# Delta keys without TensorE: their sums of squares and their turned block by VectorE and DRAM

## The chip, the cores and the metric

The kernel runs on one core of a Trainium2 chip. The metric is the device time of one execution in microseconds (us). An execution computes the whole two-layer trunk for one sequence of 256 positions. Besides timed executions there is one that was profiled; its trace gives the start and the length of every instruction on the engines TensorE (PE, with its weight loads as PEld), VectorE (DVE), ScalarE (ACT), GpSimd (POOL) and SyncE (SP).

## What is computed

The reference is a decoder trunk of two layers. Each layer is a half-step SwiGLU, a layer norm, three mixers side by side (a gated delta rule, sliding-window attention, attention to a memory), a merge, a layer norm, another half-step SwiGLU and a layer norm. The change lies in the delta rule, whose queries, keys and values come out of a short causal convolution and a SiLU; queries and keys are then scaled to unit length per position and head:

```python
def deltanet_branch(q, k, v, b, a, z, conv_w, a_log, dt_bias, norm_w):
    qkv = jax.nn.silu(causal_depthwise_conv(jnp.concatenate([q, k, v], axis=-1), conv_w))
    q, k, v = jnp.split(qkv, 3, axis=-1)          # each then (B, 256, 4 heads, 128)
    q = q * lax.rsqrt(jnp.sum(q * q, -1, keepdims=True) + RMS_EPS)
    k = k * lax.rsqrt(jnp.sum(k * k, -1, keepdims=True) + RMS_EPS)
    beta = jax.nn.sigmoid(b)
    g = -jnp.exp(a_log) * jax.nn.softplus(a + dt_bias)
    o = gated_delta_rule(q, k, v, g, beta)
    ...
```

The delta rule works on chunks. Its decays come from cumulative sums of `g` along the sequence, and the state that passes from the first block of 128 positions to the second is a product of the first block's keys, with positions as rows, and its values.

## The kernel before

All activations stand with channels on the 128 partitions and positions along the free axis, so the keys are `kT`, a tile of 128 channels x 4 heads x 256 positions. Where the kernel needs positions on the partitions, it turns 128x128 blocks.

**Weights.** All weights come as one stream of units of 128x1024 float32. For each unit SP starts a load into `raw` (four buffers, line 115). `split` (line 124) then makes two rounded parts of it: ScalarE casts it to `whi`, and VectorE subtracts, giving `wlo`, each in a ring of five buffers. Every product of a float32 pair is made of three TensorE matmuls of such parts (`mm3`). So each unit costs ScalarE one cast and VectorE one subtraction, and a buffer of the ring comes free when TensorE has used its unit. In the stage of this change a unit is 24 matmuls.

**Order.** From `mixers` on, TensorE's instructions are pinned to the order of the program's text (`pinned`, line 131). The other engines' orders are made by a scheduler when the program is built, from dependencies and priorities; each engine then takes its instructions strictly in that order. `weave(work, steps)` (line 145) lets the matmuls of `work` run unit by unit and calls the functions of `steps[n]` after the n-th unit; this places their TensorE instructions between those units. `tc.issue_after(x)` asks the scheduler for a place behind `x`.

**The stage of the change.** `conv(seg, dst)` (line 545) projects one segment in two halves of two units each. For each half, ScalarE scales and VectorE adds three shifted products (line 553) for each of two channel blocks, and ScalarE applies SiLU (line 554), whose last instruction is kept in `silu[0]`. The segments are run in the order keys, queries, values. After the third unit of the queries `tok_k` (line 577) is called:

- `tok` (line 566) turns all four heads of one 128-position block of the keys on TensorE into a PSUM tile `sm`, four transposes (line 137) for each of two blocks;
- `sumsq` (line 572) squares that on ScalarE and sums over channels on VectorE, into `ssq[:, 0]`, one number per position and head;
- the first block's turned keys are also copied by ScalarE into `ktok`;
- then `rk2` (the reciprocal of the sums) and `kn` (their square root's inverse, by small VectorE steps, lines 261 to 266) follow.

After the convolutions come the small operations of the gates: `be` (sigmoid; ScalarE's exponential at line 651 is asked to stand behind `silu[0]`, the last SiLU), `cS` (`be` times `rk2`), and a series for the softplus in `spz` and `spp` (lines 657 to 674), which ends in `g` (line 676). TensorE goes on with the projection of the cross-attention's queries and of the sliding window's keys (split into `swk`, line 866) and queries. In the latter, after its first unit, stands `decay` (line 680): its two small matmuls read `g`, and VectorE then scales `ktok` (line 689). `spread`, `products` and the recurrence follow; `rec_s1` reads `ktok`.

**What exists already for queries and values.** The queries' sums of squares are made without TensorE: `leave_q` (line 618) squares with ScalarE, turns 32x32 squares with VectorE, sums, and sends the partial sums (16 KB) to DRAM and back in four slices, whose total `land_q` takes. The values are turned by `leave_v` and `back_v`: VectorE turns 32x32 squares, four transfers put the squares in place in DRAM, and one brings the block back, with the channels in the order of squares (a, head, i) in place of (head, a, i). These transfers are started by POOL.

Of the kernel before, what the change touches and what calls it, by code (L numbers as in the profile page):

```python
# [13 lines left out]
AF = mybir.ActivationFunctionType  # L14
# [3 lines left out]
P = 128  # L18
# [20 lines left out]
def tile_trunk(ctx, tc, x, xT, mem, memT_, wst, lnp, memln, cvw, rows, cst, out):  # L39
# [33 lines left out]
    def sm():  # L73
        return T(psS, [P, 512], "sm")
# [61 lines left out]
    def transpose(*a):  # L136
        return pe(nc.tensor.transpose(*a))  # L137
# [386 lines left out]
    def mixers(l, hT, mkT, mv_, post):  # L524
# [91 lines left out]
        turned_v, sums_q = [], []  # L616

        def leave_q():
            part = T(p2, [P, 4, 8], "oqs")
            for tb in range(2):  # L620
                sq = T(p2, [P, 512], "t2", bufs=4)
                nc.scalar.activation(sq.rearrange("p (q h j) -> p q h j", q=4, h=4), squares(qT, tb), AF.Square)
                z = T(p2, [P, 512], "t2", bufs=4)
                nc.vector.transpose(z, sq)
                nc.vector.tensor_reduce(part[:, :, tb * 4:tb * 4 + 4], z.rearrange("p (q h i) -> p q h i", q=4, h=4), axis=AX.X, op=ALU.add)
            d = T(pd, [4, 32, 4, 8], "tq")
            nc.gpsimd.dma_start(d.rearrange("a j t x -> (a j) t x"), part)
            sums_q.append(T(p2, [P, 4, 8], "oqr"))
            for t in range(4):
                nc.gpsimd.dma_start(sums_q[0][32 * t:32 * t + 32], d[:, :, t].rearrange("a j x -> j a x"))  # L630

        def land_q():
            nc.vector.tensor_reduce(ssq[:, 1].rearrange("p t h -> p (t h)"), sums_q[0].rearrange("p a x -> p x a"), axis=AX.X, op=ALU.add)
# [46 lines left out]
        def decay():  # L680
# [342 lines left out]
        def branch(n, o):  # L1023
# [36 lines left out]
            8: [double, lambda: held(leave_q)]})  # L1060
        weave(branch(1, oS), {
            1: [double],
            2: [rec_v0],
# [178 lines left out]
```

## Time and profile before

| | us |
|---|---|
| median of 3 runs | 1273.09 (1271.39 to 1273.2) |
| the profiled execution | 1271.84 |
| its span, first to last instruction | 1270.1 |
| the 16 transposes of the keys, mean of one | 0.27 |
| reduction of one block's squares (line 575), x4 | 0.67 |
| copy of the turned block (line 582), x2 | 0.59 |

The page of a profile gives first the busy time of each engine, then slices of the span, the DMA queues, the chain of work that ended last, and the costliest groups. A row of the timeline gives the start and the length in us, the engine, the line, the operation, the tiles (written <- read), shapes, the count of merged instructions and, in brackets, how long the engine stood idle before it and what ended that. Neighbouring instructions of an engine overlap a little, so distances from start to start say more than lengths. A row of windows gives a stretch, its length, and for each engine the busy time in it with the count of instructions, then the granted TensorE clock, the DMA engines' busy share and GB/s.

### The profile page before, as it was taken

The page shows a single profiled execution, that of the slowest core. Times are in us where ns is not written, and L with a number is a line of the kernel's source. Part 1 is how long each engine was busy: PE and PEld are TensorE (multiplying, and loading weights), DVE is VectorE, ACT ScalarE, POOL GpSimd, SP SyncE. Part 2 cuts the span into 40 slices and gives each one's busy share as a digit, 9 for nine tenths or more (in the row PEclk, how much of TensorE's full clock was granted, in tenths as well). Part 3 has the DMA queues.
Part 4 walks back from the last instruction along what each step waited for, and adds up shares of the span by engine and source line. Part 5 has one row for each costly group of instructions (what it writes and reads, how often), then busy time and mean ns, then how long its engine had stood idle before and what let it go on. Part 6 is the DMA issues. An engine that isn't in the chain of part 4 may idle for free.

```text
span 1270.1 us, 18774 instructions
## 1 busy us (share of the span) xinstructions
PE 1258.1 (99%) x6916; PEld 1070.9 (84%) x6916; DVE 871.3 (69%) x1284; ACT 661.5 (52%) x982; POOL 221.0 (17%) x395
## 2 busy tenths in 40 slices
PE   9999999999999999999999999999999999999997
PEld 7888889999878888888888888899987788888886
DVE  6678576886667776665666665759776588766565
ACT  6456444655664544454454554455646654454441
POOL 1233000002331102221012220000023401122100
PEclk9999999999999999999999999999999999999999
DMA  8988765655554648787668887566554456578771
GB/s 293 322 265 286 249 210 160 205 179 137 164 151 150 240 139 258 243 242 220 215 208 246 256 255 216 178 185 212 162 158 133 134 189 226 174 248 243 240 231 74
DMA packets 78795, 263.56 MB, mean 208 GB/s; under 512 B 12528, under 2 KB 13968, under 8 KB 78704
## 3 DMA queue, kind: packets, MB, share of 16 engines
q1 hardware_dynamic: 66320, 232.40, 56.5%
q0 software_dynamic: 12240, 29.84, 8.7%
q8 instruction: 54, 0.88, 0.3%
q14 instruction: 37, 0.30, 0.1%
q10 hardware_dynamic: 144, 0.13, 0.0%
HBM read 247.48 MB, written 14.85 MB: 207 GB/s over the span
## 4 chain that ended last, share of the span: by engine, by line
PE 94%; DVE 3%; DMA 2%; ACT 1%; issue 1%; SPq 0%; DVEq 0%; ACTq 0%
PE acc L134 83%; PE at L134 3%; PE sm L134 3%; DMA raw<-in_wst_dram 2%; PE sm L137 1%; DVE wlo L125 1%; PE acc L335 1%; PE acc L332 1%; PE at L137 1%; PE acc L333 1%; ACT whi L125 1%; DVE h L291 0%; DVE h L296 0%; DVE h L418 0%; DVE bnst L277 0%
## 5 line engine op out<-in xcount | busy, mean ns | idle before, releaser
L125 DVE TENSOR_TENSOR wlo<-raw,whi 128x1024 fp32r<-128x1024 f32 (+2 forms) x405 | 487.1, 1210 | 277.0 <-ACT whi L125 275.0
L125 ACT CAST whi<-raw 128x1024 fp32r<-128x1024 f32 (+2 forms) x405 | 413.7, 1029 | 403.5 <-PE acc L134 314.8
L134 PE MATMUL acc<-whi,hT 128*128 128x512 f32 (+1 forms) x1824 | 563.1, 386 | 0.0
L134 PEld LDWEIGHTS acc<-whi,hT 128*128 128x128 f32 x1824 | 340.5, 188 | 68.9 <-issue 1.6
L134 PE MATMUL acc<-wlo,hT 128*128 128x512 f32 (+1 forms) x912 | 350.5, 384 | 0.1
L134 PE MATMUL acc<-whi,u 128*128 128x512 f32 x812 | 259.6, 392 | 0.0
L134 PEld LDWEIGHTS acc<-wlo,hT 128*128 128x128 f32 x912 | 171.6, 188 | 33.4 <-DVE wlo L125 0.9
L134 PEld LDWEIGHTS acc<-whi,u 128*128 128x128 f32 x812 | 152.3, 188 | 32.0 <-DVE u L125 0.5
L134 PE MATMUL acc<-wlo,u 128*128 128x512 f32 x406 | 158.2, 390 | 0.0
L362 POOL DMA_DIRECT2D tr<-t x176 | 96.0, 552 | 306.4 <-DVE t L356 299.4
L134 PE MATMUL acc<-hT,whi 128*128 128x256 f32 x672 | 121.8, 284 | 0.0
L134 PEld LDWEIGHTS acc<-hT,whi 128*128 128x128 f32 x672 | 104.7, 192 | 0.0
L134 PE MATMUL acc<-hT,wlo 128*128 128x256 f32 x336 | 95.1, 283 | 0.0
L134 PEld LDWEIGHTS acc<-wlo,u 128*128 128x128 f32 x406 | 76.3, 188 | 15.5
L134 PEld LDWEIGHTS acc<-hT,wlo 128*128 128x128 f32 x336 | 64.4, 192 | 0.0
L363 POOL DMA_DIRECT2D pt<-tr x44 | 25.0, 568 | 197.3 <-DMA tr<-t 151.6
L353 ACT ACTIVATE t<-acc 128x256 f32<-128x256 f32 x88 | 33.3, 379 | 37.1 <-PE acc L134 36.9
L134 PE MATMUL acc<-u,u 128*128 128x512 f32 x186 | 46.4, 394 | 0.0
L354 DVE TENSOR_TENSOR t<-t,acc 128x256 f32<-128x256 f32 x88 | 36.6, 417 | 8.1 <-ACT t L353 3.9
L134 PEld LDWEIGHTS acc<-u,u 128*128 128x128 f32 x186 | 34.6, 188 | 7.5
L553 DVE SCALAR_TENSOR_TENSOR t<-acc,cw,t 128x255 f32<-128x255 f32 (+2 forms) x72 | 34.5, 479 | 1.1
L125 DVE TENSOR_TENSOR u<-pt,u 128x512 fp32r<-128x512 f32 x44 | 28.9, 657 | 8.1 <-ACT u L125 8.1
(245 smaller groups left out, 1165.0 us busy)
## 6 DMA issues: line engine op xcount, KB each, us to landing
raw<-in_wst_dram SPq DMA_DIRECT2D x409, 512.0 KB, 4.4
tr<-t POOLq DMA_DIRECT2D x176, 64.0 KB, 3.9
pt<-tr POOLq DMA_DIRECT2D x44, 256.0 KB, 5.1
raw<-in_wst_dram SPq DMA_DIRECT2D x16, 324.0 KB, 3.0
gB<-in_lnp_dram SPq DMA_DIRECT2D x6, 512.0 KB, 6.7
bB<-in_lnp_dram SPq DMA_DIRECT2D x6, 512.0 KB, 7.0
w<-dr POOLq DMA_DIRECT2D x4, 512.0 KB, 12.6
t<-in_xT_dram SPq DMA_DIRECT2D x4, 256.0 KB, 5.4
```

Source lines behind the costliest of these rows:

```text
L125: return nc.scalar.copy(hi, src).ins, nc.vector.tensor_tensor(lo, src, hi.bitcast(F32), op=ALU.subtract).ins
L134: return pe(nc.tensor.matmul(*a, **k))
L137: return pe(nc.tensor.transpose(*a))
L332: nc.tensor.matmul(ps, hT[0][:, k, ts], hi[:, c], start=k == 0, stop=False)
L333: nc.tensor.matmul(ps, hT[0][:, k, ts], lo[:, c], start=False, stop=False)
L335: nc.tensor.matmul(ps, hT[1][:, k, ts], hi[:, c], start=False, stop=k == KD - 1)
L353: act = nc.scalar.activation(t[:, :, tb, :], g, AF.Silu).ins
L354: ins = nc.vector.tensor_tensor(t[:, :, tb, :], t[:, :, tb, :], u, op=ALU.mult).ins
L362: nc.gpsimd.dma_start(d[:, :, q].rearrange("b c x -> c b x"), z[32 * q:32 * q + 32].rearrange("c (b x) -> c b x", b=4))
L363: back = nc.gpsimd.dma_start(y, d.rearrange("b c q x -> (b c) (q x)")).ins
L553: nc.vector.scalar_tensor_tensor(yc[:, j, d:], b[:, j, :S - d], w[:, t:t + 1], yc[:, j, d:], op0=ALU.mult, op1=ALU.add)
```

## The change

`leave_q` becomes `leave_sums(n, src)` and serves the keys too; its total becomes `total(n)`. After the third unit of the queries' projection the keys' squares and partial sums are made from `kT` and sent to DRAM and back. `leave_k` turns the first block of the keys as `leave_v` does the values, over DRAM, into a `pt` tile `kback` in the order of squares. `tok_k` now begins with `total(0)`, stands behind the third convolution in the text and is asked to stand behind the last SiLU. Line 689 reads `kback` through a view and writes `ktok` in order of heads. TensorE's transposes, `tok`, `sumsq` and the copy go.

```diff
-        def tok(src, tb):
-            ps = sm()
-            for h in range(4):
-                transpose(ps[:, h * P:(h + 1) * P], src[:, h, tb * P:(tb + 1) * P], ident)
-            return ps.rearrange("p (h e) -> p h e", h=4)
-
-        def sumsq(ps, dst):
-            sq = T(p2, [P, 4, P], "t2", bufs=4)
-            nc.scalar.activation(sq, ps, AF.Square)
-            nc.vector.tensor_reduce(dst, sq, axis=AX.X, op=ALU.add)
+        kback = []
+
+        def leave_k():
+            z = T(p2, [P, 512], "t2", bufs=4)
+            nc.vector.transpose(z, squares(kT, 0))
+            d = T(pd, [4, 32, 4, P], "tk")
+            for a in range(4):
+                nc.gpsimd.dma_start(d[:, :, a].rearrange("t j x -> j t x"), z[32 * a:32 * a + 32].rearrange("j (t x) -> j t x", t=4))
+            kback.append(T(p2, [P, D], "pt")[:, 0:512])
+            nc.gpsimd.dma_start(kback[0], d.rearrange("t j a x -> (t j) (a x)"))
 
         def tok_k():
-            for tb in range(2):
-                ps = tok(kT, tb)
-                sumsq(ps, ssq[:, 0, tb, :])
-                if tb == 0:
-                    nc.scalar.copy(ktok, ps)
+            total(0)
             nc.vector.tensor_scalar(ssq[:, 0], ssq[:, 0], RMS_EPS, None, ALU.add)
...
-        def leave_q():
+        def leave_sums(n, src):
             part = T(p2, [P, 4, 8], "oqs")
             for tb in range(2):
                 sq = T(p2, [P, 512], "t2", bufs=4)
-                nc.scalar.activation(sq.rearrange("p (q h j) -> p q h j", q=4, h=4), squares(qT, tb), AF.Square)
+                nc.scalar.activation(sq.rearrange("p (q h j) -> p q h j", q=4, h=4), squares(src, tb), AF.Square)
                 z = T(p2, [P, 512], "t2", bufs=4)
                 nc.vector.transpose(z, sq)
                 nc.vector.tensor_reduce(part[:, :, tb * 4:tb * 4 + 4], ...)
             d = T(pd, [4, 32, 4, 8], "tq")
             nc.gpsimd.dma_start(d.rearrange("a j t x -> (a j) t x"), part)
-            sums_q.append(T(p2, [P, 4, 8], "oqr"))
+            sums_q[n] = T(p2, [P, 4, 8], "oqr")
             for t in range(4):
-                nc.gpsimd.dma_start(sums_q[0][32 * t:32 * t + 32], d[:, :, t].rearrange("a j x -> j a x"))
+                nc.gpsimd.dma_start(sums_q[n][32 * t:32 * t + 32], d[:, :, t].rearrange("a j x -> j a x"))
+
+        def total(n):
+            nc.vector.tensor_reduce(ssq[:, n].rearrange("p t h -> p (t h)"), sums_q[n].rearrange("p a x -> p x a"), axis=AX.X, op=ALU.add)
...
         weave(conv(1, kT), {})
-        weave(conv(0, qT), {3: [tok_k]})
+        weave(conv(0, qT), {3: [lambda: leave_sums(0, kT), leave_k]})
         weave(conv(2, vT), {})
+        with tc.issue_after(silu[0]):
+            tok_k()
...
-            nc.vector.tensor_tensor(ktok, ktok, ks.unsqueeze(2).to_broadcast([P, 4, P]), op=ALU.mult)
+            nc.vector.tensor_tensor(*(t.rearrange(r, a=4, h=4) for t, r in ((ktok, "p h (a i) -> p a h i"), (kback[0], "p (a h i) -> p a h i"))), ks.unsqueeze(1).unsqueeze(3).to_broadcast([P, 4, 4, 32]), op=ALU.mult)
```

On TensorE and SP nothing else moves: TensorE's list has lost the eight transposes per layer, SP's is the same. The scheduler's orders of the other engines differ around this stage, in both layers alike. Three places follow, from the first layer; numbers behind names tell buffers apart, and those of before and after differ.

ScalarE at the last SiLU of the values (`u8` is `vT`), before; `whi_493` and `whi_503` are casts of weight units, `u4` is a part of the cross-attention's queries:

```order
L125 CAST whi_493_2787<-raw_492_2786 128x1024
L125 CAST u4_461_2579<-acc_468_2586 128x512
L554 ACTIVATE u8_387_2076<-t2_446_2531 128x512
L651 ACT_TABLE_LOAD
L651 ACTIVATE be_447_2541<-ba_382_2061 128x8
L125 CAST whi_503_2857<-raw_502_2856 128x1024
L661 ACTIVATE spe_450_2549<-spe_450_2549 128x8
L125 CAST whi_507_2894<-raw_506_2893 128x1024
L125 CAST u4_461_2579<-acc_475_2649 128x512
L125 CAST whi_516_2944<-raw_515_2943 128x1024
L125 CAST swk0_99<-acc_482_2712 64x256 x2
L125 CAST whi_532_3061<-raw_531_3060 128x1024
```

and after:

```order
L125 CAST u4_467_2590<-acc_474_2597 128x512
L125 CAST whi_509_2868<-raw_508_2867 128x1024
L125 CAST whi_513_2905<-raw_512_2904 128x1024
L554 ACTIVATE u8_387_2076<-t2_451_2526 128x512
L652 ACT_TABLE_LOAD
L652 ACTIVATE be_453_2552<-ba_382_2061 128x8
L662 ACTIVATE spe_456_2560<-spe_456_2560 128x8
L125 CAST whi_522_2955<-raw_521_2954 128x1024
L125 CAST u4_467_2590<-acc_481_2660 128x512
L125 CAST swk0_99<-acc_488_2723 64x256
L125 CAST whi_538_3072<-raw_537_3071 128x1024
L125 CAST swk0_99<-acc_488_2723 64x256
```

The casts of two more units (`whi_503` and `whi_507` of before are `whi_509` and `whi_513` now) stand ahead of the SiLU and of `be` behind it, and the cast `whi_532` of before, now `whi_538`, stands between the two `swk` casts.

VectorE ahead of `g`, before; `spp` is the softplus series, `wlo` a weight unit's subtraction, `u6` a part of the cross-attention's queries:

```order
L125 TENSOR_TENSOR u6_462_2580<-acc_475_2649,u4_461_2579 128x512
L671 SCALAR_TENSOR_TENSOR spp_453_2558<-spp_453_2558,spz2_452_2556 128x8 x3
L672 SCALAR_TENSOR_TENSOR spp_453_2558<-spp_453_2558,spz_451_2552 128x8
L673 TENSOR_SCALAR spp_453_2558<-spp_453_2558 128x8
L674 SCALAR_TENSOR_TENSOR spp_453_2558<-spt_449_2547,spp_453_2558 128x8
L125 TENSOR_TENSOR wlo_517_2945<-raw_515_2943,whi_516_2944 128x1024
L676 TENSOR_TENSOR g_454_2569<-spp_453_2558,nea_96 128x8
L125 TENSOR_TENSOR swk1_100<-acc_482_2712,swk0_99 64x256 x2
L125 TENSOR_TENSOR wlo_533_3062<-raw_531_3060,whi_532_3061 128x1024
```

and after:

```order
L672 SCALAR_TENSOR_TENSOR spp_459_2569<-spp_459_2569,spz2_458_2567 128x8
L125 TENSOR_TENSOR swk1_100<-acc_488_2723,swk0_99 64x256
L672 SCALAR_TENSOR_TENSOR spp_459_2569<-spp_459_2569,spz2_458_2567 128x8 x2
L125 TENSOR_TENSOR wlo_539_3073<-raw_537_3071,whi_538_3072 128x1024
L672 SCALAR_TENSOR_TENSOR spp_459_2569<-spp_459_2569,spz2_458_2567 128x8
L125 TENSOR_TENSOR swk1_100<-acc_488_2723,swk0_99 64x256
L673 SCALAR_TENSOR_TENSOR spp_459_2569<-spp_459_2569,spz_457_2563 128x8
L674 TENSOR_SCALAR spp_459_2569<-spp_459_2569 128x8
L675 SCALAR_TENSOR_TENSOR spp_459_2569<-spt_455_2558,spp_459_2569 128x8
L677 TENSOR_TENSOR g_460_2580<-spp_459_2569,nea_96 128x8
```

Both `swk` subtractions and the unit that was `wlo_533` (now `wlo_539`) have moved from behind `g` to ahead of it.

VectorE at the sums of squares of the keys, before; `t2_417` is a convolution of the queries, `t2_423` and `t2_425` are squares:

```order
L125 TENSOR_TENSOR wlo_445_2503<-raw_443_2501,whi_444_2502 128x1024
L553 SCALAR_TENSOR_TENSOR t2_417_2286<-acc_410_2225,cw_92,t2_417_2286 128x255
L575 TENSOR_REDUCE ssq_388_2077<-t2_423_2332 128x4
L553 SCALAR_TENSOR_TENSOR t2_417_2286<-acc_410_2225,cw_92,t2_417_2286 128x254
L575 TENSOR_REDUCE ssq_388_2077<-t2_425_2341 128x4
L553 SCALAR_TENSOR_TENSOR t2_417_2286<-acc_410_2225,cw_92,t2_417_2286 128x253
L583 TENSOR_SCALAR ssq_388_2077<-ssq_388_2077 128x8
L125 TENSOR_TENSOR wlo_471_2589<-raw_469_2587,whi_470_2588 128x1024
L584 RECIPROCAL rk2_391_2080<-ssq_388_2077 128x8
```

and after; `oqr` are the four slices read back, `t2_435` is a convolution of the queries, `t2_443` one of the values:

```order
L125 TENSOR_TENSOR wlo_484_2663<-raw_482_2661,whi_483_2662 128x1024
L553 SCALAR_TENSOR_TENSOR t2_435_2384<-acc_418_2296,cw_92,t2_435_2384 128x255
L553 SCALAR_TENSOR_TENSOR t2_443_2455<-acc_436_2394,cw_92,t2_443_2455 128x255
L553 SCALAR_TENSOR_TENSOR t2_435_2384<-acc_418_2296,cw_92,t2_435_2384 128x254
L125 TENSOR_TENSOR wlo_487_2693<-raw_485_2691,whi_486_2692 128x1024
L553 SCALAR_TENSOR_TENSOR t2_435_2384<-acc_418_2296,cw_92,t2_435_2384 128x253
L553 SCALAR_TENSOR_TENSOR t2_443_2455<-acc_436_2394,cw_92,t2_443_2455 128x254
L629 TENSOR_REDUCE ssq_388_2077<-oqr_428_2340 128x8
L553 SCALAR_TENSOR_TENSOR t2_443_2455<-acc_436_2394,cw_92,t2_443_2455 128x253
L579 TENSOR_SCALAR ssq_388_2077<-ssq_388_2077 128x8
L580 RECIPROCAL rk2_391_2080<-ssq_388_2077 128x8
```

Where the reductions stood in one half of the queries' convolution, the total (line 629) now stands among the values' convolutions, ten convolution steps and three units' subtractions behind the second of the reductions that feed it (line 621).

More of the change, by code (lines that the diff above doesn't have):

```diff
@@ L614, in land_v @@
                 late["dve"] = nc.vector.tensor_tensor(vin[:, tb], vin[:, tb], kn[:, tb, :].unsqueeze(1).unsqueeze(3).to_broadcast([P, 4, 4, 32]), op=ALU.mult).ins
-        turned_v, sums_q = [], []
-        def leave_q():
+        turned_v, sums_q = [], {}
+        def leave_sums(n, src):
             part = T(p2, [P, 4, 8], "oqs")
@@ L627, in leave_q @@
             nc.gpsimd.dma_start(d.rearrange("a j t x -> (a j) t x"), part)
-            sums_q.append(T(p2, [P, 4, 8], "oqr"))
+            sums_q[n] = T(p2, [P, 4, 8], "oqr")
             for t in range(4):
-                nc.gpsimd.dma_start(sums_q[0][32 * t:32 * t + 32], d[:, :, t].rearrange("a j x -> j a x"))
+                nc.gpsimd.dma_start(sums_q[n][32 * t:32 * t + 32], d[:, :, t].rearrange("a j x -> j a x"))
+        def total(n):
+            nc.vector.tensor_reduce(ssq[:, n].rearrange("p t h -> p (t h)"), sums_q[n].rearrange("p a x -> p x a"), axis=AX.X, op=ALU.add)
         def land_q():
-            nc.vector.tensor_reduce(ssq[:, 1].rearrange("p t h -> p (t h)"), sums_q[0].rearrange("p a x -> p x a"), axis=AX.X, op=ALU.add)
+            total(1)
             nc.vector.tensor_scalar(qeps, ssq[:, 1], RMS_EPS, RMS_EPS * P, ALU.add, ALU.mult)
         weave(conv(1, kT), {})
-        weave(conv(0, qT), {3: [tok_k]})
+        weave(conv(0, qT), {3: [lambda: leave_sums(0, kT), leave_k]})
         weave(conv(2, vT), {})
+        with tc.issue_after(silu[0]):
+            tok_k()
         sh = [P, 2, 4]
@@ L1059, in mixers @@
             7: [double, lambda: w_values(1), lambda: held(land_v)],
-            8: [double, lambda: held(leave_q)]})
+            8: [double, lambda: held(lambda: leave_sums(1, qT))]})
         weave(branch(1, oS), {
```

## The prediction

> **What bounds the kernel now.** I read the page's first and fourth parts, then windows, then the timeline of each engine around the changed place.
>
> ```profile
> span 1270.1 us, 18774 instructions
> PE 1258.1 (99%) x6916; PEld 1070.9 (84%) x6916; DVE 871.3 (69%) x1284; ACT 661.5 (52%) x982; POOL 221.0 (17%) x395
> ...
> PE 94%; DVE 3%; DMA 2%; ACT 1%; issue 1%; SPq 0%; DVEq 0%; ACTq 0%
> ...
> 240.00:280.00 40.00, 40.00 (x337) 39.99 (x336) 35.84 (x81) 25.07 (x38) 1.44 (x2) 1.00 0.61 179
> ```
>
> The first lines are the page's span, busy times and chain; the last is a window over the convolutions of the first layer (stretch, sum, then PE, PEld, DVE, ACT, POOL, the clock, the DMA share, GB/s). PE is the bound, so work taken off PE counts one to one, and work put elsewhere counts only if PE ends up waiting for it. The average hides one thing: VectorE, 69% busy overall, is at 35.84 of 40 us here. Room for more of its work is small exactly where the change puts it.
>
> **What is removed.** PE's timeline around the eight transposes of the first layer (start, duration, engine, line, operands, count):
>
> ```profile
> 245.62 0.28 PE L134 MATMUL acc<-hT,wlo 128*128 128x256 f32 x1
> ...
> 245.98 0.28 PE L134 MATMUL acc<-hT,wlo 128*128 128x256 f32 x1
> 246.10 1.03 PE L137 MATMUL sm<-cs,u 128*128 128x128 f32 x8
> 246.89 0.48 PE L134 MATMUL acc<-hT,whi 128*128 128x256 f32 x2
> 247.21 0.28 PE L134 MATMUL acc<-hT,wlo 128*128 128x256 f32 x1
> ```
>
> Three matmuls normally take 0.36 us (245.62 to 245.98). With the transposes between them the same step takes 247.21 - 245.98 = 1.23 us. So 0.87 us goes from PE per layer, **-1.74 us** for both. ScalarE loses one copy per layer; it has idle time, so that is worth nothing.
>
> **Where PE needs the moved work.** Nobody on PE reads the turned keys or their sums at once. The first matmul behind them in PE's fixed order that reads a small VectorE result is `decay` (line 683), which reads `g`. Its weight load, VectorE's way to `g`, and ScalarE's way to `be`, from which that way starts:
>
> ```profile
> 278.60 0.52 PEld L134 LDWEIGHTS sm<-g,cs 128*128 128x128 f32 x4
> ...
> 268.28 1.23 DVE L125 TENSOR_TENSOR wlo<-raw,whi 128x1024 fp32r<-128x1024 f32 x1 [0.23 <-ACT whi L125]
> 269.42 0.68 DVE L125 TENSOR_TENSOR u<-acc,u 128x512 fp32r<-128x512 f32 x1
> 270.81 0.17 DVE L652 TENSOR_SCALAR be<-be 128x8 f32<-128x8 f32 x1 [0.71 <-ACT be L651]
> ...
> 276.66 0.17 DVE L672 SCALAR_TENSOR_TENSOR spp<-spp,spz 128x8 f32<-128x8 f32 x1
> 276.86 0.17 DVE L673 TENSOR_SCALAR spp<-spp 128x8 f32<-128x8 f32 x1
> 277.06 0.17 DVE L674 SCALAR_TENSOR_TENSOR spp<-spt,spp 128x8 f32<-128x8 f32 x1
> 277.17 1.23 DVE L125 TENSOR_TENSOR wlo<-raw,whi 128x1024 fp32r<-128x1024 f32 x1
> 278.32 0.16 DVE L676 TENSOR_TENSOR g<-spp,nea 128x8 f32<-128x8 f32 x1
> 278.39 0.41 DVE L125 TENSOR_TENSOR swk<-acc,swk 64x256 fp32r<-64x256 f32 x1
> ...
> 267.20 1.05 ACT L125 CAST whi<-raw 128x1024 fp32r<-128x1024 f32 x1 [1.46 <-PE acc L134]
> 268.15 0.58 ACT L125 CAST u<-acc 128x512 fp32r<-128x512 f32 x1
> 268.62 0.63 ACT L554 ACTIVATE u<-t 128x512 f32<-128x512 f32 x1
> ...
> 272.96 1.05 ACT L125 CAST whi<-raw 128x1024 fp32r<-128x1024 f32 x1 [1.13 <-PE acc L134]
> ...
> 275.84 1.05 ACT L125 CAST whi<-raw 128x1024 fp32r<-128x1024 f32 x1 [1.35 <-PE acc L134]
> ```
>
> `g` ends at 278.48 and PE takes it at 278.60, 0.12 us later: **no slack today**. After the change PE is there 0.87 us sooner, at 277.73, so even an unchanged `g` makes PE give its gain back. And `g` gets later, for two reasons that the built order shows; I work out both.
>
> First, the weight step in front of `g`. The casts at 272.96 and 275.84 are released by PE, one per unit of 2.88 us, so the next unit's buffer comes free at 278.72, when PE ends the unit just before `decay`. Before, that unit's cast and its `wlo` stand behind `g`. Now the cast stands between the two `swk` casts, and the `wlo`, the second `swk` subtraction and four small operations stand ahead of `g`. So the cast starts at 278.72 - 0.87 = 277.85; its `wlo` 1.08 later (267.20 to 268.28), at 278.93; the next operation 1.14 after that (268.28 to 269.42), at 280.07. Operations that don't feed each other overlap by 0.09 (1.23 against 1.14), so the small one next takes 0.08 (0.17 less 0.09) and the `swk` 0.32; then three small ones and `g` follow at a pitch of 0.20 (276.66 to 277.06): `g` starts at 281.07 and ends at 281.23. PE goes on 0.12 later, at 281.35. This floor has no term that VectorE's speed elsewhere could remove: PE waits for a conversion that PE itself releases 0.1 us earlier.
>
> Second, the activation in front of `be`. `be` follows the last SiLU (L554) of the values. Before, that SiLU runs at 268.62, behind the cast released at 267.20. Now two more casts stand ahead of it; the second is released two units later, at 267.20 + 5.76 - 0.87 = 272.09, and the SiLU starts 0.95 behind it, at 273.04. `be` on VectorE keeps its distance of 2.19 us (268.62 to 270.81): 275.23. From there to the `wlo` of the first reason the order has six chained operations on `spz` and `spp` at a pitch of 0.20, with those on `be` between them (1.2 us); a `wlo` (1.14); a `u` subtraction (0.59); a `swk` (0.32); four small ones (about 0.5). That is 3.75 us: the `wlo` starts at 278.98, 0.05 later than by the first reason. Both reasons give the same place, so taking one away leaves the other.
>
> PE goes on at 281.35 to 281.40 where it went on at 278.60: +2.8 us per layer, the saving already in it (a wait of 3.65 less 0.87). The second layer is the same program with the same distances:
>
> ```profile
> 897.12 0.63 ACT L554 ACTIVATE u<-t 128x512 f32<-128x512 f32 x1
> ...
> 906.82 0.16 DVE L676 TENSOR_TENSOR g<-spp,nea 128x8 f32<-128x8 f32 x1
> ...
> 907.13 0.57 PE L134 MATMUL sm<-g,cs 128*128 128x8 f32 x4
> ```
>
> SiLU to `g` is 9.70 us in both layers. Sum: 2 x 2.8 = **+5.6 us**. Nothing behind `decay` takes it back: what PE runs next is PE-bound, and every operand there moves along with `g`.
>
> **The other added work.** VectorE gets three transposes and one small reduction per layer; the two reductions of the sums stay two. ScalarE keeps two squares. POOL gets ten DMA issues. Nearest rows: a convolution, the same operations for the queries, and POOL's idle time at this place.
>
> ```profile
> 245.52 1.51 DVE L553 SCALAR_TENSOR_TENSOR t<-acc,cw,t 128x255 f32<-128x255 f32 x3
> ...
> 371.85 1.29 DVE L624 STREAM_TRANSPOSE t<-t 128x512 f32<-128x512 f32 x2
> ...
> 374.76 0.68 DVE L625 TENSOR_REDUCE oqs<-t 128x16 f32<-128x512 f32 x1
> ...
> 375.73 0.54 POOL L627 DMA_DIRECT2D tq<-oqs  x1 [11.13 <-DVE oqs L625]
> ...
> 379.89 2.21 POOL L630 DMA_DIRECT2D oqr<-tq  x4 [1.40 <-DMA tq<-oqs]
> ...
> oqr<-tq POOLq DMA_DIRECT2D x8, 4.0 KB, 1.8
> ...
> 278.56 2.04 POOL L716 TENSOR_TENSOR w<-cs,g 128x512 f32<-128x512 f32 x2 [48.63 <-DVE g L676]
> ```
>
> Three transposes at 0.65 and 0.2 us are 2.1 us of VectorE. The cover: casts come one per 2.88 us as PE frees one of five buffers, so PE reaches a converted unit four units (11.5 us) after its cast started, and cast plus subtraction take 2.3; a lag of 9 us hides. If that cover were gone the price is 2.1 us per layer. POOL idles 48.63 us up to L716, which waits for `g`; ten issues at 0.55 lie in that. The turned keys are read only behind `decay`, by a scaling of the same size as before: nothing. SP's order is the same.
>
> The new wait is L629, VectorE's total over four reloaded slices; behind it in VectorE's order stand weight subtractions and the convolutions, for which PE and ScalarE wait. The three convolution steps at 245.52 take 0.50 each, chained; mixed with other work less, so I estimate 0.45. The last slice sum ends near 252.7: 245.52 plus four steps (1.8), two `wlo` (2.28), three transposes at 0.64, two reductions at 0.59. The round trip by the query rows is 4.16 (375.73 to 379.89), three issue pitches (1.65) and 1.8 to landing: 7.6 us, so 260.3. VectorE reaches L629 at 260.6 (ten steps, three `wlo` more) and `be`'s place at 274.4 (0.2, ten steps, five `wlo`, one `u`, 14 small ones at 0.20), 0.8 before ScalarE allows it. So 1.1 us may be added unseen. From below the trip is free; from above `tq` waits for three 64 KB transfers just ahead in its queue, at worst their whole landing time:
>
> ```profile
> tr<-t POOLq DMA_DIRECT2D x176, 64.0 KB, 3.9
> ```
>
> That would be 3.9 - 1.1 = 2.8 us per layer. I take free, the query row being the same operation.
>
> **Clock.** The last matmul is over by 1262; windows behind it (same columns):
>
> ```profile
> 1262.00:1266.00 4.00, 0.00 (x0) 0.00 (x0) 3.79 (x11) 0.29 (x1) 0.00 (x0) 1.00 0.00 0
> 1266.00:1270.10 4.10, 0.00 (x0) 0.00 (x0) 0.62 (x2) 0.00 (x0) 0.00 (x0) 0.56 0.35 128
> ```
>
> PE idle for 4 us keeps clock 1.00; beyond that it falls. My wait is 3.65 us, just inside, so the sum has no term for it and stays at +5.6. The Trainium skill (TensorE: Matmul & The Clock Gate, section "What's actually happening") says the clock halves after one idle window of about 3.4 us, with windows that run freely; by it a wait of 3.65 would seldom hold a whole window, and where it did, half speed for one window would add 1.7 us per layer and give +9.0. The end of this trace agrees that the clock falls with idling but puts it later; no idle stretch inside the program shows it.
>
> **Rivals.** (1) *Not slower:* `g` is on time and only the transposes go. It decides at 277.73 for the first layer; for that the conversion ahead of `g` must not wait for PE's last unit (as if a sixth buffer were free) and the SiLU must start 3.6 us sooner than worked out. For it: ScalarE is 52% busy. Against: the rows "<-PE acc" and the order. Price: -1.74, so 1271.4 beside the median; 10%. (2) *The total's round trip is late:* it decides at 8.7 us; at the worst above, 2.8 per layer, it adds 5.6: 1283.6. The transfers ahead in the queue speak for it, the rows of the queries against; 12%. (3) *The clock falls in the wait*: how long it stays low no row shows; if as long as the 4 us of idling that it took, PE loses half of that, 2 us per layer: 1282; 8%. That transposes would stay on PE is out: its built list has lost them and nothing else.
>
> **Numbers.** The profiled execution took 1271.84 us, 1.7 more than its span; plus 5.6 is 1277.4. The median of the three runs is 1273.09, which gives 1278.7. I take 1278.0; 70% for the forecast, 1275.5 to 1280.5. The range reaches into (2) and (3): 1275 to 1284. What can be told from no change is about 0.2%, 2.5 us. Faster by that: 3%, since the whole removal is 1.74. Within it: 9%, case (1). Slower: 88%.
>
> **What would show it.** Right: at `decay` PE waits 3 to 4 us for DVE `g` in both layers; the SiLU of the last values starts some 4 us later; the `wlo` ahead of `g` waits for a cast that PE released; L629 waits little. Wrong: no wait at `decay`, a wait at L629 or in the convolutions on PE, or a clock below 1.00 behind `decay`.

## The result, and the profile after

| | before | after |
|---|---|---|
| median, us (lowest to highest) | 1272.24 (1270.21 to 1273.2), 4 runs | 1287.28 (1286.22 to 1287.91), 4 runs |
| the profiled execution | 1271.84 | 1286.7 |

The ratio is 1.0118, with an interval of 1.0105 to 1.0131: the changed kernel is slower by 15 us, where 1278.0 was forecast in a range up to 1284.0. A second set of runs of the same kernel, told below, had 1283.73 (ratio 1.0106, 1.0089 to 1.0123).

From the page of after: the span, the busy engines, the granted clock in 40 slices, and the chain of work that ended last.

```profile
span 1284.9 us, 18783 instructions
PE 1265.3 (98%) x6900; PEld 1077.0 (84%) x6900; DVE 875.2 (68%) x1292; ACT 660.1 (51%) x980; POOL 232.1 (18%) x415
...
PEclk9999999989999999999999999999898999999999
...
PE 87%; DVE 4%; DMA 4%; POOL 3%; issue 2%; ACT 1%; DVEq 0%; POOLq 0%; ACTq 0%
```

PE has 16 matmuls fewer and is nevertheless busy for 7 us more: the matmuls themselves have become longer. The PEclk row says why: three slices show 8 where before every slice had 9. The ninth slice begins 257 us into the span, the 29th and the 31st at 899 and 964 us.

The waits of after (what waited on what: us in total, times, the longest) have a pair that before did not have:

```profile
PEld sm L134 <- DVE g L677: 8.0, 2, 4.1
PE sm L134 <- DVE g L677: 7.6, 2, 3.9
```

The timeline of after at that place in the first layer, engine by engine (start, length, engine, line, operation, tiles; idle time before it in brackets):

```profile
281.54 0.72 PEld L134 LDWEIGHTS sm<-g,cs 128*128 128x128 f32 x3 [3.90 <-DVE g L677]
...
252.64 0.57 POOL L623 DMA_DIRECT2D tq<-oqs  x1 [0.41 <-DVE oqs L621]
...
256.00 2.17 POOL L626 DMA_DIRECT2D oqr<-tq  x4 [2.25 <-DMA tq<-oqs]
...
261.40 0.21 DVE L629 TENSOR_REDUCE ssq<-oqr 128x8 f32<-128x32 f32 x1 [0.71 <-DMA oqr<-tq]
...
272.05 0.47 DVE L553 SCALAR_TENSOR_TENSOR t<-acc,cw,t 128x253 f32<-128x253 f32 x1
...
273.09 1.23 DVE L125 TENSOR_TENSOR wlo<-raw,whi 128x1024 fp32r<-128x1024 f32 x1
275.14 0.17 DVE L653 TENSOR_SCALAR be<-be 128x8 f32<-128x8 f32 x1 [0.83 <-ACT be L652]
...
278.92 1.23 DVE L125 TENSOR_TENSOR wlo<-raw,whi 128x1024 fp32r<-128x1024 f32 x1
...
280.25 0.43 DVE L125 TENSOR_TENSOR swk<-acc,swk 64x256 fp32r<-64x256 f32 x1
...
281.32 0.17 DVE L677 TENSOR_TENSOR g<-spp,nea 128x8 f32<-128x8 f32 x1
...
272.01 1.05 ACT L125 CAST whi<-raw 128x1024 fp32r<-128x1024 f32 x1 [1.83 <-PE acc L134]
272.96 0.63 ACT L554 ACTIVATE u<-t 128x512 f32<-128x512 f32 x1
...
277.77 1.04 ACT L125 CAST whi<-raw 128x1024 fp32r<-128x1024 f32 x1 [0.87 <-PE acc L134]
```

The last SiLU of the values runs at 272.96 (268.62 before), the subtraction ahead of `g` at 278.92, `g` at 281.32, and PE, which had read `g` at once before, stands still until 281.54. The total of the sums (L629) waited 0.71 us.

That wait cannot be 15 us. The rest is seen in windows whose edges are put on the clock's changes. Within a trace these changes lie whole multiples of 3.41 us apart; "grid" below means the row of 3.41 us windows that runs through them (columns: a stretch, its length, busy time of PE, PEld, DVE, ACT, POOL with counts, granted clock, DMA share, GB/s):

```profile
277.18:280.59 3.41, 0.67 (x6) 0.46 (x4) 3.34 (x10) 1.41 (x2) 0.00 (x0) 1.00 0.57 180
280.59:287.42 6.83, 5.88 (x27) 5.88 (x28) 2.29 (x8) 0.18 (x1) 2.03 (x2) 0.50 0.28 81
...
912.05:915.47 3.42, 0.04 (x1) 0.04 (x1) 3.12 (x12) 0.85 (x2) 0.01 (x1) 1.00 0.67 180
915.47:922.30 6.83, 6.83 (x32) 6.83 (x33) 1.54 (x3) 0.89 (x2) 2.02 (x2) 0.50 0.17 64
980.32:983.73 3.41, 1.89 (x31) 0.72 (x31) 3.38 (x5) 1.45 (x2) 0.00 (x0) 1.00 0.88 308
983.73:990.56 6.83, 6.83 (x63) 5.61 (x58) 2.31 (x6) 2.01 (x8) 0.00 (x0) 0.50 0.55 192
```

Three times the clock is at 0.50 for 6.83 us: in and behind both waits at `decay`, and once in the second layer behind another wait of PE, 1.52 us at `w_values` (L780's result; 1.04 us before), that is followed by small 32x32 matmuls. What a fall costs is read from PE's rows around the third, first at full speed, then at 0.50:

```profile
978.22 0.62 PE L134 MATMUL acc<-whi,hT 128*128 128x512 f32 x2
978.91 0.62 PE L134 MATMUL acc<-whi,hT 128*128 128x512 f32 x2
...
986.19 1.05 PE L134 MATMUL acc<-whi,hT 128*128 128x512 f32 x2
987.47 1.05 PE L134 MATMUL acc<-whi,hT 128*128 128x512 f32 x2
```

Three matmuls (two of these and one between them) take 0.69 us at full speed and 1.28 at 0.50; three of 128x256 take 0.36 and 0.64 (283.21 to 283.85). So a low stretch loses some 0.44 of PE's time in it. PE is busy for 5.88 + 6.83 + 6.83 = 19.54 us of the three, so they cost an estimated 8.6 us. The two waits less the transposes are 7.6 - 1.74 = 5.8, and the wait at `w_values` is 0.5 longer: together 14.9, as between the profiled executions (1286.7 - 1271.84).

### The profile page after: what moved, and what is told of

It is laid out like the page before. It is cut to its first block, busy times and chain, and to the rows that moved or that the text cites. A ratio compares the mean times of both kernels' runs of the same rounds, so it can differ in the third digit from the quotient of the medians.

```text
span 1284.9 us, 18783 instructions
## 1 busy us (share of the span) xinstructions
PE 1265.3 (98%) x6900; PEld 1077.0 (84%) x6900; DVE 875.2 (68%) x1292; ACT 660.1 (51%) x980; POOL 232.1 (18%) x415
## 4 chain that ended last, share of the span: by engine, by line
PE 87%; DVE 4%; DMA 4%; POOL 3%; issue 2%; ACT 1%; DVEq 0%; POOLq 0%; ACTq 0%
PE acc L134 77%; PE at L134 3%; PE sm L134 3%; DVE wlo L125 2%; DMA w<-dr 2%; PE sm L137 1%; POOL t L846 1%; PE acc L332 1%; PE acc L333 1%; POOL l L837 1%; PE acc L335 1%; POOL t L847 1%; DMA dr<-t 1%; DMA raw<-in_wst_dram 1%; ACT whi L125 0%
## 5 line engine op out<-in xcount | busy, mean ns | idle before, releaser
L134 PE MATMUL acc<-hT,whi 128*128 128x256 f32 x672 | 125.9, 290 | 0.0
L134 PEld LDWEIGHTS acc<-hT,whi 128*128 128x128 f32 x672 | 108.5, 198 | 0.0
L125 DVE TENSOR_TENSOR u<-pt,u 128x512 fp32r<-128x512 f32 x44 | 28.9, 657 | 11.1 <-ACT u L125 11.1
L1039 POOL TENSOR_TENSOR u<-u,gt 128x512 f32<-128x512 f32 x16 | 20.7, 1293 | 78.2 <-DVE gt L1037 74.3
```

Source lines behind the costliest of these rows:

```text
L125: return nc.scalar.copy(hi, src).ins, nc.vector.tensor_tensor(lo, src, hi.bitcast(F32), op=ALU.subtract).ins
L134: return pe(nc.tensor.matmul(*a, **k))
L1039: nc.gpsimd.tensor_tensor(mg[tb][:, js], mg[tb][:, js], gt[tb][:, js], op=ALU.add)
```

## The experiments

Theory C: the order of the work costs about 5.6 us, as forecast, and falls of the clock the rest. The rivals hold that the added VectorE work, the transfers or the wait cost the 15 us by themselves. All ratios are to the kernel before, run on the same chip. "Wait" is PE's whole wait for `g` in the profiled execution, "low" its time at 0.50 before the end of the program.

| run | what it is | median, us | ratio (interval) | wait, us | low, us |
|---|---|---|---|---|---|
| fill | after, PE kept busy at `decay` | 1277.62 | 1.0052 (1.0040 to 1.0065) | 0.7 | 0 |
| half_fill | the same, half as long | 1280.92 | 1.0068 (1.0048 to 1.0089) | 4.4 | 6.8 |
| late | after, `decay` later on PE | 1269.49 | 0.9988 (0.9979 to 0.9996) | 0 | 0 |
| before_late | before, `decay` later on PE | 1270.91 | 1.0000 (0.9991 to 1.0009) | 0 | 0 |
| slow5 | before, `g` later by 5 operations | 1277.26 | 1.0036 (1.0023 to 1.0049) | 3.0 | 0 |
| slow10 | before, `g` later by 10 operations | 1282.66 | 1.0087 (1.0072 to 1.0103) | 7.2 | 10.2 |
| sums | the sums' half of the change | 1282.39 | 1.0092 (1.0074 to 1.0110) | 7.4 | 10.2 |
| turn | the turned block's half | 1284.49 | 1.0102 (1.0085 to 1.0119) | 7.4 | 13.7 |
| both_reasons | after, both reasons taken away | 1284.32 | 1.0102 (1.0087 to 1.0118) | 9.3 | 13.7 |
| one_reason | after, the first taken away | 1279.87 | 1.0064 (1.0048 to 1.0080) | 5.5 | 10.2 |
| after_again | after itself | 1283.73 | 1.0106 (1.0089 to 1.0123) | 7.4 | 10.2 |

**fill: keep PE busy where it idled.**

```diff
         def decay():
             ps = sm()
             gf = g.rearrange("p t h -> p (t h)")
+            for _ in range(28):
+                matmul(ps[:, 128:384], xt[0](0)[:, 0:P], xt[0](0), start=True, stop=True)
             matmul(ps[:, 0:8], tri, gf, start=True, stop=True)
```

> The changed kernel with 28 matmuls of 128x256 (about 0.12 us each, 3.4 us in all, results never read) put into PE's order just ahead of the matmul that needs g, so that PE works where it idled 3.7 and 3.9 us. g itself comes no sooner. Theory C (the clock): of the changed kernel's +15 us about 5.6 are the two waits and the rest is time at clock 0.50 behind PE's idling. Then the records show no fall at decay, PE still goes on at about 281.3 in the first layer, and the time is 1278 us, or 1281 if the third fall, at the wait in w_values of the second layer, stays. Rival W (the added VectorE work, the transfers and the wait cost the 15 us by themselves): 1287 with a clock of 1.00 throughout.

Windows of fill on its own clock's grid (the first over the added matmuls, the second over the wait at `w_values`), and the timeline's row of the weight load that reads `g`:

```profile
278.23:281.64 3.41, 3.41 (x31) 3.41 (x30) 3.34 (x10) 1.42 (x2) 0.00 (x0) 1.00 0.62 179
...
974.55:977.96 3.41, 1.90 (x10) 0.94 (x8) 3.38 (x5) 0.96 (x1) 0.00 (x0) 1.00 1.01 294
```

```profile
282.72 0.52 PEld L134 LDWEIGHTS sm<-g,cs 128*128 128x128 f32 x4 [0.54 <-DVE g L677]
```

`g` is as late as in the changed kernel, PE reaches the work behind it no sooner (282.72 here, in a trace that runs 1.2 us later from its start on: PE's last matmul ahead of this place starts at 278.74 in place of 277.57), and the time falls from 1287.28 (1283.73 in the second set) to 1277.62. The clock stays at 1.00, at `w_values` too. So useless work on PE saves 7 to 8 us by the ratios (1.0118 and 1.0106 against 1.0052), and what is left, 0.0052 x 1271.05 = +6.6 us (5.1 to 8.3), is the order's own cost. The two traces also price the falls: matmul by matmul, after drops back against fill by 2.6, 3.0 and 3.0 us across its three low stretches, 8.6 in all, as estimated above. Rival W is out.

**late: let PE have something else to do.**

```diff
         weave(halves(xt, use_sq), {
-            1: [decay],
-            2: [lambda: spread(0), lambda: x_scores(0)],
-            3: [lambda: spread(1)],
-            4: [lambda: products(0, 0), lambda: products(0, 1)]})
+            2: [lambda: x_scores(0), decay],
+            3: [lambda: spread(0)],
+            4: [lambda: spread(1), lambda: products(0, 0), lambda: products(0, 1)]})
```

> The changed kernel with decay put one step later in PE's order, behind x_scores(0), the first spread and the second moved one step on; the same operations. PE has work of its own (x_scores) while g is finished. Theory C (waits of 2.8 us per layer net, and falls of the clock behind them): both go, what is left is the 8 transposes per layer less on PE, 1270.5 to 1271.5 us, just under the kernel before; 1274 if the fall at w_values of the second layer stays. Rival W (the added VectorE work costs by itself, wherever decay stands): 1278 or more.

```profile
281.91 0.17 DVE L677 TENSOR_TENSOR g<-spp,nea 128x8 f32<-128x8 f32 x1
...
282.46 0.53 PEld L134 LDWEIGHTS sm<-g,cs 128*128 128x128 f32 x4
```

VectorE's order ahead of `g` has not changed, and `g` ends 0.4 us ahead of the load, which has no idle time in brackets (0.17 us in the second layer). 1269.49 is the fastest median of this study. It lies 1 us below the 1270.5 to 1271.5 that were expected; the kernel before, at 1271.05 in these runs, is 1.2 us below its 1272.24 of the first set too. The added VectorE work and the ten transfers per layer cost nothing that can be seen as soon as PE doesn't stand behind `g`.

**before_late: is late's gain the transposes or the placing?** The same edit in the kernel before.

> The kernel before with only the placing of the run named late: decay behind x_scores(0), the first spread and the second one step on. Nothing of the change. If late's small gain over the kernel before comes from the removed transposes (8 per layer, 0.87 us): 1271 us, the kernel before within 0.1%. If it comes from the placing: 1269.5, as late. A wait of its own (x_scores earlier, spread later) would show as 1273 or more.

The ratio is 1.0000, within 0.0009 (1.1 us) either way. So the placing alone shows no gain, and what late gains, 0.0012 x 1271.05 = 1.5 us (0.5 to 2.7), fits the change's own worth, for which 1.74 was worked out. The times alone do not prove it, for the intervals of the two runs overlap slightly.

**slow5 and slow10: the wait without the change.** The kernel before, with `n` of 5 or 10:

```diff
         nc.vector.tensor_tensor(g, pp, rowb(nea[:, l, :]), op=ALU.mult)
+        for _ in range(n):
+            nc.vector.tensor_scalar(g, g, 1.0, None, ALU.mult)
```

> The kernel before, nothing of the change, with 5 small VectorE operations on g (times 1.0), chained, so that g comes about 1 us later and PE waits for it some 1.5 us per layer. Theory C: an idle of 1.5 us with dense work on both sides brings no fall of the clock; 1275.3 us (+3.0), clock 1.00. Rival F (any new idle at decay lets the clock fall): two falls of about 3 us more, 1281.

> The kernel before with 10 such operations on g, so that PE waits some 3.6 us per layer at decay, as long as in the changed kernel, but with none of the change's operations and transfers. Theory C: the waits cost 7.3 us and the clock falls to 0.50 in both of them, about 3 us each: 1285.5 us. Rival W (the changed kernel's own work causes what the waits don't explain): no fall, 1279.5.

The first layer and the second of slow10, then the second layer of slow5, in windows on each kernel's grid:

```profile
279.78:283.19 3.41, 0.48 (x5) 0.51 (x5) 2.58 (x9) 0.83 (x1) 0.55 (x1) 1.00 0.59 160
283.19:286.60 3.41, 3.41 (x17) 3.41 (x18) 1.69 (x3) 0.18 (x1) 1.50 (x2) 0.50 0.42 142
...
911.25:914.66 3.41, 1.01 (x9) 0.80 (x7) 3.18 (x12) 1.41 (x2) 0.00 (x0) 1.00 0.61 203
914.66:921.49 6.83, 5.65 (x26) 5.68 (x27) 2.43 (x7) 0.18 (x1) 2.04 (x2) 0.50 0.24 80
```

```profile
909.04:912.45 3.41, 1.90 (x16) 1.73 (x16) 3.07 (x11) 1.67 (x3) 0.06 (x1) 1.00 0.57 189
```

slow10 has none of the change's work and falls in both waits, so a wait of 3.6 us is enough by itself. Its first fall lasts 3.41 us, its second 6.83, so the sum comes out smaller than expected: 7.2 of waiting and 0.44 of 3.41 + 5.65 make 11.2 us; 0.0087 x 1271.05 is 11.1. The profiled execution of slow5 idles 1.5 us per layer and doesn't fall. Its time is a partial miss: five executions lie at 1274.0 and 1274.5 and at 1277.3 to 1278.2, and the profiled one (1277.26), of the upper group, is already 1.4 us late 38 us into the span, where the edit has done nothing yet. Only the two low ones are as expected; what parts the groups was not followed up. The granted clock of the whole span, which takes in the low end of the program, is 0.998 and 0.999 in the two low ones, 0.998 in the profiled one and 0.996 in the other two. So no fall made the profiled one late, but that the other two had one somewhere cannot be excluded.

**sums and turn: which half of the change does it?** sums turns the first block with four TensorE transposes and a copy again; turn makes the sums from eight TensorE transposes at the third unit of the queries again, and keeps `leave_k`.

```diff
# sums
-            nc.vector.transpose(z, squares(kT, 0))
...
+            for h in range(4):
+                transpose(ps[:, h * P:(h + 1) * P], kT[:, h, 0:P], ident)
+            nc.scalar.copy(ktok, ps.rearrange("p (h e) -> p h e", h=4))
# turn
-            total(0)
+            for tb in range(2):
+                sumsq(tok(kT, tb), ssq[:, 0, tb, :])
...
-        weave(conv(0, qT), {3: [lambda: leave_sums(0, kT), leave_k]})
+        weave(conv(0, qT), {3: [tok_k, leave_k]})
         weave(conv(2, vT), {})
-        with tc.issue_after(silu[0]):
-            tok_k()
```

> The sums half of the change alone: sums of squares by VectorE, POOL's transfers and total(0) behind the third convolution; the first block of the keys is turned by four TensorE transposes and copied by ScalarE, as before. Theory O (the wait at decay comes from the order in which ScalarE and VectorE do their work once tok_k has left the third unit of the queries, and the clock falls in it): PE waits 3.7 us for g in each layer and the clock falls there, about 1283 us (1271 + 6.5 + two falls of 3). Rival T (it is the turned block's transfers and its VectorE transpose that make g late): no wait, 1270 to 1271.

> The other half alone: the turned block over DRAM as in the change; the sums of squares as before, from eight TensorE transposes at the third unit of the queries, so no transfer of sums and no wait of VectorE for one. Theory O: here too the order of ScalarE's casts ahead of the last SiLU moves, PE waits 3.7 us for g in each layer, 1284 us (1271 + 7.4 + two falls of 3). Rival R (the round trip of the sums, the total waiting for it, delays VectorE and so g): no wait, 1271 to 1272.

The waits of sums, then of turn:

```profile
PE sm L134 <- DVE g L674: 7.4, 2, 3.7
```

```profile
PE sm L134 <- DVE g L687: 7.4, 2, 3.7
```

Each half alone brings the whole wait and the falls. turn has no round trip of the sums at all, so rival R is out; sums has no turned block, so rival T is out. turn calls `tok_k` where the kernel before did and waits all the same, so the wait does not hang on moving that call, which Theory O named. In both the order is that of the changed kernel: the last weight subtraction and both `swk` stand ahead of `g`.

**one_reason and both_reasons: the prediction's two reasons.** A weight unit is held behind an instruction by asking for a place behind it. `hold` is read in `unit`, numbered from the end of the convolutions. one_reason has only the entry for unit 11. The lines are shortened; names inside the brackets stand for the instructions:

```diff
+                    for b in mine:          # mine = hold.pop(made[0], [])
+                        held.enter_context(tc.issue_after(b))
...
+        hold[b0 + 8] = [be_exponential, cS_product]
+        hold[b0 + 9] = [softplus_exponential, spz2_product]
...
+        hold[b0 + 11] = [g_product, second_swk_cast]
```

> The changed kernel with only the first reason taken away: the weight unit that PE releases last is cast behind both swk casts and subtracted behind g. The prediction's step (two reasons give the same place, taking one away leaves the other): PE still waits 3.6 us or more for g, 1284 to 1287 us with the clock's falls. Rival Q (what stands ahead of g on VectorE adds up, so every subtraction that leaves is worth about its 1.1 us): a wait of 2.6 us per layer, 1275 without a fall, 1278 to 1282 with falls of one or two windows.

> The changed kernel with both reasons of the prediction taken away by order alone: the cast and subtraction of the weight unit that PE releases last (the 11th behind the convolutions) are put behind g on VectorE and behind the swk casts on ScalarE; the two casts that stood ahead of the last SiLU go behind the exponentials of be and of the softplus, their subtractions behind cS and spz2, as before the change. If the two reasons are all: no wait at decay, clock 1.00, 1270 to 1271 us. Rival V (VectorE's own order: its last convolution step of the values stands 4 us later than before, behind other work, and the SiLU waits for that): a wait of 3.5 to 4 us stays, 1277 without falls of the clock, 1283 with two.

one_reason's wait, then both_reasons' (timeline of the load; the waits of both in the table above), and ScalarE's and VectorE's rows of both_reasons at the last SiLU:

```profile
281.48 0.84 PEld L140 LDWEIGHTS sm<-g,cs 128*128 128x128 f32 x4 [2.85 <-DVE g L684]
```

```profile
283.59 0.93 PEld L140 LDWEIGHTS sm<-g,cs 128*128 128x128 f32 x4 [4.76 <-DVE g L686]
...
272.37 0.48 DVE L559 SCALAR_TENSOR_TENSOR t<-acc,cw,t 128x253 f32<-128x253 f32 x1
...
272.94 0.63 ACT L560 ACTIVATE u<-t 128x512 f32<-128x512 f32 x1 [2.47 <-DVE kn L272]
```

Without the first reason PE waits 2.8 us in place of 3.8: rival Q, not the prediction's "taking one away leaves the other". Without both the wait is longer, not gone. This trace runs 1.2 us later from its start on than that of after (PE's last matmul ahead of the wait starts at 278.75 in place of 277.57), so the SiLU at 272.94 is 1.2 us sooner by PE's place than in after. It is not back where it was before, some 3 us sooner still: the two casts no longer stand ahead of it, and ScalarE idles 2.47 us, but VectorE's last convolution step ends only at 272.37 + 0.48 = 272.85. That is rival V: a third reason, which the prediction didn't work out (before, that step ended at 266.54 + 1.51 = 268.05). From `be` to `g` VectorE then takes 8.2 us (275.13 to 283.37) in place of 6.2, because the held subtractions run between the steps of the softplus; that is more than the sooner SiLU gives. The edit moved work as well as took reasons away, so it shows that the third reason is there, not what it costs alone, and no run here takes the whole wait away by VectorE's or ScalarE's order.

**half_fill: how much idling is too much?** fill with 14 matmuls in place of 28.

> The kernel with fill matmuls at decay, with 14 in place of 28, so that PE idles about 2.0 us in each decay in place of 3.7. Nothing else. Clock by a whole idle window: no fall, 1278 us as with 28. Rival H (a fall comes as soon as a window of the clock's grid is mostly idle; after idle windows of a busy share of 0.30 or less the clock fell, and at 0.56 it stayed up twice and fell once): 2.0 us idle leaves a window at least 0.41 busy, so none or one fall, 1278 to 1281; two falls, 1284, would put the threshold above 0.41.

```profile
278.45:281.86 3.41, 1.39 (x12) 1.19 (x11) 2.56 (x9) 0.46 (x2) 0.56 (x1) 1.00 0.69 214
281.86:285.27 3.41, 3.41 (x18) 3.41 (x18) 1.75 (x3) 0.18 (x1) 1.47 (x2) 0.50 0.22 84
...
913.33:916.74 3.41, 1.04 (x9) 0.95 (x9) 2.33 (x8) 0.20 (x2) 0.92 (x1) 1.00 0.70 231
916.74:920.15 3.41, 3.41 (x18) 3.41 (x18) 1.66 (x3) 0.00 (x0) 1.11 (x2) 0.50 0.11 44
```

Two falls, each of 3.41 us, after windows in which PE was busy for 1.39 and 1.04 of 3.41 us. At 0.44 of 3.41 us each they are 3.0; the medians of half_fill and fill differ by 3.3. The times' intervals overlap, so the clock rows carry this, not the medians. Neither expectation named this outcome: two falls, but short ones. Nor does every execution have them: one of the four took 1276.63 us at a granted clock of 0.998 over its span, as fill did (0.997 to 0.999), the others 1280.63 to 1281.45 at 0.994 to 0.996. So at an idle of some 2 us the same kernel seems to fall or not; only a trace with falls was kept.

**after_again: the same kernel, the same falls?**

> The changed kernel itself once more, to see whether its falls of the clock come again at the same places. Theory C with the clock's grid at a free phase: both waits at decay fall again, for one or two windows (3.4 or 6.8 us at 0.50) each; the fall at w_values of the second layer need not come, and then the time is about 1284 us in place of 1287. Rival: three falls of 6.8 us at the same places, 1287.

```profile
276.67:280.08 3.41, 1.01 (x9) 0.80 (x7) 3.35 (x9) 1.46 (x3) 0.00 (x0) 1.00 0.70 214
280.08:286.91 6.83, 5.54 (x26) 5.54 (x27) 2.64 (x8) 0.18 (x1) 2.04 (x2) 0.50 0.32 94
911.55:914.96 3.41, 0.18 (x2) 0.18 (x2) 2.98 (x11) 0.87 (x2) 0.15 (x1) 1.00 0.71 178
914.96:918.37 3.41, 3.41 (x17) 3.41 (x18) 1.67 (x3) 0.18 (x1) 1.88 (x2) 0.50 0.33 130
```

Both falls at `decay` come again, the second one short, and the third doesn't come: 0.44 of 5.54 + 3.41 is 3.9 us in place of 8.6. The profiled executions, 1281.59 and 1286.7, differ by 5.1. The granted clock of the whole span is 0.990 or 0.991 in all four executions of the first set and 0.993 to 0.995 in the four of this one, against 0.996 to 0.999 in the kernel before's. So the falls are part of the changed kernel, but their number and length are not fixed: the waits are the same, the phase of the clock's grid is not.

## Why the prediction was wrong

- **The transposes: right.** -1.74 us. PE's last matmul ahead of `decay` starts at 277.57 in after and 278.52 in before, 0.95 sooner; 0.09 of that is there ahead of the transposes already (245.89 against 245.98), so 0.86 per layer, forecast 0.87. The gain of late, 1.5 us, fits.
- **The wait at `decay`: right, in place and size.** 3.65 us forecast, 3.8 measured. The SiLU was put at 273.04 (272.96), `be` at 275.23 (275.14), the last subtraction at 278.93 to 278.98 (278.92), `g` at 281.07 (281.32). Without falls the whole is +6.6 us (fill, 5.1 to 8.3), against +5.6.
- **"Taking one away leaves the other": wrong.** The first reason is worth 1 us of the 3.8 (one_reason). Behind the second stands VectorE's last convolution step, 4.5 us later than before. VectorE's arrival at `be`'s place had been worked out rightly (274.4; the subtraction ahead of `be` ends at 273.09 + 1.23 = 274.32), but the SiLU needs VectorE earlier, at that convolution, and this chain was left out. It didn't change the time.
- **The other added work: right.** L629 was to be reached at 260.6 and to wait little; it waits 0.71 us, up to 261.40. The round trip was longer than the estimate of 7.6 us (252.64 to 261.40 is 8.8), just past the point where rival 2 was to decide; turn, without a round trip, has the same wait, so it decided nothing.
- **The clock: the step that failed.** "PE idle for 4 us keeps clock 1.00 ... My wait is 3.65 us, just inside, so the sum has no term for it." The rows behind it began at 1262 and 1266. Taken on the grid on which the clock changes, the same end of the kernel before reads:

```profile
1263.04:1266.45 3.41, 0.00 (x0) 0.00 (x0) 3.30 (x9) 0.29 (x1) 0.00 (x0) 1.00 0.00 0
1266.45:1270.10 3.65, 0.00 (x0) 0.00 (x0) 0.17 (x1) 0.00 (x0) 0.00 (x0) 0.50 0.39 144
```

The clock went down at the end of the first window that was empty on the grid; the idling before 1263.04 fell into a window that was busy for most of its length. So the row told where one window ended, not how long PE may idle. A wait of 3.8 us leaves some window empty for at least half of the wait, 1.9 of 3.41 us, wherever the grid lies, and in every trace here with such a wait the fall came. So the term that the sum had at nothing is the one that failed: in its place the three falls cost 8.6 us. Rival 3 had the mechanism, with a chance of 8% and 2 us per fall; measured were 2.6 and 3.0 us at `decay`, and a third fall of 3.0 us elsewhere that nothing in the forecast had named.

The rule of the Trainium skill (TensorE: Matmul & The Clock Gate, "What's actually happening") that was weighed there gave +9.0. Its windows of some 3.4 us that run freely are what the rows show; that a fall needs a window that is idle throughout, as the prediction took it, is not: windows with 1.39 and 1.04 us of PE work preceded falls too. The +9.0 also took one window per fall; 11 of the 17 falls in these traces lasted two.

## What to carry to other kernels

Where TensorE is the bound and waits for nothing, the price of a new wait is not its length: from some 2 us on it can also bring a clock of 0.50 for one or two windows of 3.41 us, so that 7.2 to 7.6 us of waiting in two places came with a loss of 11 to 15. Waits of 2.0 and 2.4 us fell in half_fill's trace, though probably not in each of its executions; waits of 1.5 us between dense work did not fall in slow5's, but 1.52 us followed by small matmuls did once, in after. Look first for work that TensorE can do meanwhile: here a few lines of its order (late) turned 1.2% slower into 0.1% faster, and even useless matmuls were better than idling. And before a row of windows is used to say when a clock falls, find the times at which the clock changes, and put the windows' edges there. Before a time in one trace is set against a time in another, find out how far apart the two traces already are: by 15 us into the span the traces here already differed by up to 2.0 us.

## What the runs showed of the hardware

Within each trace every change of the granted clock lies a whole number of 3.41 us from every other, and the grid's phase differs from execution to execution. In the eight traces with falls in the middle of the program, all 16 windows in which PE was busy for 0.44 of the time or less were followed by a fall (from 0.00 in both_reasons to 1.51 of 3.41 us in turn's second layer, below). At the end of the program the clock falls in all 13 traces: 11 times behind an empty window, and behind one with 1.03 us of PE work in fill and 1.39 in one_reason. One window of after_again there, with 1.54 us (0.45, from 1269.95), was not followed by a fall. Of the six windows at 0.56 to 0.62 in the middle of the program one was followed by a fall (980.32 of after, 1.89 us, most of its matmuls 32x32) and the others not (1.90 us in fill and in slow5, above). So for dense work the limit may lie as close as between 0.44 and 0.45; that one fell at 0.56 shows that PE's busy share is not the whole rule.

```profile
914.19:917.60 3.41, 1.51 (x13) 1.30 (x11) 3.38 (x9) 1.96 (x4) 0.00 (x0) 1.00 0.51 168
```

The low stretch lasted two windows wherever PE was not busy throughout the first of them (8 of 8). Where it was, it lasted one window 6 times and two windows 3 times; what decides there stays open. Why the build's order comes out so differently for either half of the change was not tried.
